# Two groups of dilated values projected together: 512 columns per strided stationary load, in two passes over h

## The chip, the cores and the metric

The kernel runs on 1 core of one Trainium2 chip. The metric is the device time of one execution in microseconds (us); lower is better. Each time shown is a run of the whole program; one further execution was recorded by the hardware profiler, and all rows below come from that one.

## The reference, cut to what matters

The program computes two transformer-like models in a row. Only the first is touched here: two layers over 512 tokens, each with a normed input h (512 x 1024), latent attention of 8 heads, and dilated attention of 8 heads in three groups.

```python
DIL_PAIRS = ((128, 1), (512, 4), (2048, 16))     # window, dilation
...
h = rms_norm(x, norm_g[layer])
p = h @ w_in[layer]
c_q, c_kv, k_r, gate_a, dil_qkv, gate_b = jnp.split(p, split_points, axis=-1)
a = mla_attention(c_q, c_kv, k_r, ...) * jax.nn.silu(gate_a)
b = dilated_attention(dil_qkv, cos_d, sin_d) * jax.nn.silu(gate_b)
x = x + jnp.concatenate([a, b], axis=-1) @ w_out[layer]
...
qkv = dil_qkv.reshape(B, S, DIL_GROUPS, 3, DIL_HEADS, DIL_HD)
for g, (window, dil) in enumerate(DIL_PAIRS):
    ...
    v = qkv[:, :, g, 2]
    o, lse = banded_attention(to_strided(q, dil), to_strided(k, dil), to_strided(v, dil), window // (2 * dil))
```

The values v of a group are a plain product of h with 512 columns of `w_in` (8 heads of 64). Groups 1 and 2 want them with the tokens in strided order.

## The kernel before, in words

All products of the first model are made of exact splits: a number is a high part plus a low part, and `mm3` (lines 346 to 351) issues three matmuls for each pair of operands, high by high at line 349, high by low at 350 and low by high at 351. The normed input lies feature-major in two tiles named `big` (high and low), 8 chunks of 128 features by 512 tokens. Each matmul has its own load of the stationary operand, which the profile lists as PEld LDWEIGHTS. A load takes 128 tokens by 128 features; the moving operand is the weights, in tiles `whi` and `wlo`.

`vproj(half)` projects the dilated values of four heads (256 columns) of each group. A call of `tile(g, i)` makes one tile of 128 tokens: 8 chunks by 3 matmuls of 256 columns into a PSUM bank of tag `mm` (three banks). For group 0 the tokens are 128 neighbours. For groups 1 and 2 they are every fourth token from i on, so the stationary load reads `big` with a step of four elements, 16 bytes. The first tile of a group also calls `k.weights` twice: each call is a DMA of 512 KB, a copy on ScalarE (line 400, the high part) and a subtraction on VectorE (line 401, the low part). ScalarE empties the bank at line 620 (groups 1 and 2) or 624 (group 0).

```python
sl = slice(i, 512, 4) if g else slice(i * P, (i + 1) * P)
for c in range(8):
    w, o = ws[g][c // 4], (c % 4) * 256
    k.mm3(acc[:, 0:256], tok(c, sl), (w[0][:, o : o + 256], w[1][:, o : o + 256]), c == 0, c == 7)
```

The steps of `vproj` are (cost, step) pairs. In each layer `v0` (first four heads) gives four steps ahead of the transposition of the latents (`latent`, lines 712 to 718), two more between those transpositions, and the rest to the first two of eight fills; `v1` gives four steps to the fourth fill and eight to the sixth. A fill is spread by `weave` between eight units of attention: `scores` (scores on TensorE, minimum on VectorE, exponential on ScalarE, scale on VectorE), and two units later `transposed`. TensorE and SyncE run in the order of the program text; for ScalarE, VectorE and GpSimd a scheduler orders the instructions. VectorE also carries work of the second model that `k.weights` pulls in, one step per call as a rule: products with `in_mw` at lines 953 and 954. `values` multiplies the finished values with the attention's weights, much later. Tiles of tag `v4` (ten slots) hold the values.

Of the kernel before, what the change touches and what calls it, by code (L numbers as in the profile page):

```python
# [30 lines left out]
# ---------------------------------------------------------------- host side  # L31
def _kp(w):
    """[K, N] -> [128, K/128, N], row k*128+p at partition p."""
    k, n = w.shape
    return w.reshape(k // P, P, n).transpose(1, 0, 2)
# [16 lines left out]
def layout(inp):  # L52
    """Rearranges the inputs' elements (copies only)."""
# [7 lines left out]
    for L in range(2):  # L61
# [3 lines left out]
        for half in range(2):  # L65
            for g in range(3):
                c0 = 1184 + ((g * 3 + 2) * 8 + 4 * half) * 64
                vs.append(wk[:, :, c0 : c0 + 256])
# [97 lines left out]
def constants():  # L166
    """Tables that depend on shapes alone."""
# [62 lines left out]
# tags of what outlives block 1's attention, and of what the even mixer starts with  # L230
# [3 lines left out]
# (t, g): t = 0 for q, 1 for k  # L234
# [4 lines left out]
# ---------------------------------------------------------------- chip side  # L239
class Phase:  # L240
    """Opens the pools of one stretch of the program, in the order of their bytes:
    one for each list of tags and, unless it is None, one for the rest."""
# [27 lines left out]
class K:  # L270
# [17 lines left out]
    def t(self, shape, tag, bufs, dt=F32):  # L288
        """A tile of the current phase's pool (weights: of the common pool)."""
        pool = self.sb if tag in ("wraw", "whi", "wlo", "cath", "catl") else self.two if tag == "big" else self.of.get(tag, self.pool)  # L290
        return pool.tile(shape, dt, tag=tag, bufs=bufs, name=self.nm(tag))
# [9 lines left out]
    def arrive(self, halves=2):  # L301
        """The next tile of x, or half of it, leaves the part before."""
        for _ in range(halves):
            if self.tail is not None:
                next(self.tail, None)

    def norms(self, first, rest):
        """first(i), then rest(i) of its result, for the tiles of x as they arrive."""
        self.arrive()
        self.arrive()  # L310
        a = first(0)
        self.arrive()
        b = first(1)
        self.arrive()
        for i in range(4):
            rest(i, a)
            a, b = b, first(i + 2) if i < 2 else None
# [5 lines left out]
    # ---- weights  # L323
# [5 lines left out]
    def weights(self, src, off, n, gate=None, raw=None, sub=None, tag=None):  # L329
        """Columns off.. of a weight array, loaded and split exactly into hi + lo."""  # L330
# [15 lines left out]
    def mm3(self, out, lhs, rhs, first, last):  # L346
        """out (+)= lhs^T rhs with lhs, rhs = (hi, lo)."""
        mm = self.nc.tensor.matmul
        mm(out, lhs[0], rhs[0], start=first, stop=False)  # L349
        mm(out, lhs[0], rhs[1], start=False, stop=False)  # L350
        mm(out, lhs[1], rhs[0], start=False, stop=last)  # L351

    def fm(self, w, nk, rhs):
        """Feature-major product: 128 columns of w against all tokens."""
# [6 lines left out]
    def copy(self, out, in_):  # L361
        """PSUM evacuation, alternating between the two engines that can."""
# [6 lines left out]
    def rsqrt(self, ss, n, eps=True):  # L369
        """[128, n] mean squares -> 1/sqrt(. + eps)."""  # L370
# [35 lines left out]
    def norm_steps(self, xn, hT, i):  # L406
        """xn [128 tokens, 1024] -> hT[:, :, tokens of tile i], split."""
# [18 lines left out]
def both(*gens):  # L426
    """Their steps in turn."""
    for _ in zip_longest(*gens):
        pass


def slow(gen, n):
    """Its steps with n - 1 empty ones after each."""
# [5 lines left out]
def weave(units, fill):  # L439
    """Emits the units with the fill's (cost, step) pairs spread evenly between them."""  # L440
# [9 lines left out]
def block1_layer(k, L, x, hT):  # L450
# [3 lines left out]
    # ---- norm and transposition  # L454
# [9 lines left out]
    def wc_weights(half):  # L464
        """The first chunks lie in other slots: they are split before the last part's end."""
# [84 lines left out]
    # Steps of dense work, as (cost, step): they fill the attention's waits.  # L550

    # ---- dilated q and k of a pair of heads, feature-major, with rope
# [51 lines left out]
    # ---- dilated values of four heads, token-major  # L604
    def vproj(half):
# [3 lines left out]
        def tile(g, i):  # L609
            if i == 0:  # L610
                base = (half * 3 + g) * 2048
                ws[g] = [k.weights(I["wv"][L], base + c * 1024, 1024) for c in range(2)]
                vs[g] = t([P, 4, 256], "v4", 10)
            acc = k.bank("mm")
            sl = slice(i, 512, 4) if g else slice(i * P, (i + 1) * P)
            for c in range(8):
                w, o = ws[g][c // 4], (c % 4) * 256
                k.mm3(acc[:, 0:256], tok(c, sl), (w[0][:, o : o + 256], w[1][:, o : o + 256]), c == 0, c == 7)
            if g:
                nc.scalar.activation(vs[g][:, i, :], acc[:, 0:256], AF.Copy, scale=0.5)  # L620
            else:
                # tile i holds tokens 128 i - 64 .. 128 i + 63, wrapped
                for src, dst in ((0, 64), (64, 0)):
                    nc.scalar.activation(vs[g][dst : dst + 64, (i + (src > 0)) % 4, :], acc[src : src + 64, 0:256], AF.Copy, scale=0.5)

        return [(2.6, lambda g=g, i=i: tile(g, i)) for g in (1, 2, 0) for i in range(4)]

    def gate(which, hp):
        """2 * silu(h w_gate) of a pair of heads, feature-major."""
# [29 lines left out]
    def proj(hp):  # L659
        """Queries and keys of a pair of latent heads, with their rope rows."""  # L660
# [30 lines left out]
    # ---- latent projections  # L691
# [36 lines left out]
    # rope of the shared key part  # L728
# [16 lines left out]
    # ---- latent values and the rope part of q  # L745
# [28 lines left out]
    # ---- attention: 64 units, first the latent heads', then the dilated heads'  # L774
# [3 lines left out]
    def softmax(pr, bias, src):  # L778
        """pr = exp(bias - src) / sum."""
# [57 lines left out]
    def values(p):  # L837
        """Of both heads of a pair, in turn: they take different columns of the array."""
# [7 lines left out]
        else:  # L846
            vs = vss[hp // 2]
            for g in (1, 2):
                for r in range(4):
                    for o, PT, hc in halves:  # L850
                        nc.tensor.matmul(
                            o[:, r * P : (r + 1) * P],
                            vs[g][:, r, hc],
# [67 lines left out]
def adaln(k, rows):  # L921
    """Modulation vectors of both layers (and the context's), as rows in DRAM;
    a generator, so that its steps lie between those of other work."""
# [52 lines left out]
def rms(k, src, tag=None):  # L976
    """1/rms of [128, 1024] rows; returns (scratch tile, [128, 1])."""
# [13 lines left out]
def new_cat(k, last=False):  # L991
    """A pair of blocks of w_out's left operand, split; the phase's last outlives it."""
# [24 lines left out]
def token_acc(k, ws, lhs, nk, acc=None, c0=None):  # L1017
    """lhs^T w over nk chunks of 128, or the four from c0; ws: split chunks of 4 * 256."""
# [22 lines left out]
def ctx_steps(k):  # L1041
    """The context's keys, transposed, and values, into DRAM: (cost, step) pairs."""
# [53 lines left out]
def twice(k, dst, src):  # L1096
    """Both halves of the partitions of dst = src, split."""
# [5 lines left out]
def even_mixer(k, x, rows):  # L1103
# [4 lines left out]
    # ---- the first part's last norm, the mixer's norm, and transposition  # L1108
# [5 lines left out]
    def squares(i, engine):  # L1114
        """Of x, and of x fg, which replaces it."""
# [10 lines left out]
    def rms(i):  # L1126
        """x r1 fg normed again has 1/rms = r1 rsqrt(r1^2 mean(u^2) + eps)."""
# [27 lines left out]
    # ---- keys, values, queries: T holds heads k0 k1 q0 .. q7  # L1155
# [4 lines left out]
    def finish(h0, nh):  # L1160
        """Gains, rope and norm of heads h0 .. h0+nh-1."""
# [74 lines left out]
    # ---- pooled branch  # L1236
# [5 lines left out]
    def pool_means(b, w=None):  # L1242
# [5 lines left out]
        # the window's width w times (mean - p): pool_scale is divided by w  # L1248
# [36 lines left out]
    # ---- attention: 32 units (pair of heads, tile of queries, head of the pair)  # L1285
# [40 lines left out]
    def values(u):  # L1326
        """Of both heads of a pair, whose second unit is u."""
# [22 lines left out]
    # ---- the order of the work  # L1350
# [35 lines left out]
def odd_mixer(k, x, rows):  # L1386
# [14 lines left out]
    # spatial gating operand, token-major, normed per group  # L1401
# [60 lines left out]
def router(k, L):  # L1462
    """The router's weights, and the shift's part of its logits."""
# [17 lines left out]
def moe_tables(k, L, rows):  # L1481
    """What an expert layer reads that does not depend on its input."""
# [8 lines left out]
def moe(k, L, x, tables, out):  # L1491
# [9 lines left out]
    # ---- router: x A is routed, and 1 / rms and the shift's part come to its logits  # L1501
# [19 lines left out]
    def logits(i):  # L1521
        """Four groups of the array's columns take two chunks each; their sums are added in turning them."""
# [40 lines left out]
    def route(i):  # L1563
        """Ranks within the groups' logits and within each group's experts', and the chosen two."""
# [23 lines left out]
    def before(i):  # L1588
        """How many tokens come before tile i's in their experts' lists."""
# [4 lines left out]
    def spots(i, n):  # L1594
        """The places of the tokens in their experts' lists less 256: in bfloat16, positive if not chosen."""
# [11 lines left out]
    def places(dst, e_pos, e_info, c0=0, c1=5, oh=None):  # L1607
        """One-hot matrix of each slot's token against token numbers and its weight's parts."""
# [9 lines left out]
    def indices(src, n, nm):  # L1618
        """[128, n, 2] sums -> the slots' tokens (out of bounds for an empty slot)."""
# [33 lines left out]
    def weigh():  # L1653
        """Each choice's weight, halved (the experts' activation comes doubled), in three exact parts."""
# [46 lines left out]
    def gate_up(e):  # L1701
        """The chunks of an expert's first two products."""
# [30 lines left out]
    def hidden(gu):  # L1733
        """2 silu(gate) up."""
# [84 lines left out]
    def store(y, gi):  # L1819
        """The tokens' rows += y."""  # L1820
# [32 lines left out]
    # ---- experts with more than 128 tokens: the rest of their lists  # L1853
# [53 lines left out]
    for e in range(15):  # L1907
        if e == 3 and out is None:
            # the last expert's slots, token by token
# [20 lines left out]
    # ---- the tokens' rows, what the last expert adds to them, and the odd mixer's norm  # L1930
# [44 lines left out]
def body(tc, I, out, stop=None):  # L1975
    nc = tc.nc
    with (
# [21 lines left out]
        with k.phase("two"):  # L1999
            k.two = k.pool  # L2000
            with tc.manual_schedule(engines={mybir.EngineType.PE, mybir.EngineType.SP}):
# [14 lines left out]
                # block 1's last steps and the even mixer's first ones overlap  # L2016
# [52 lines left out]
```

## Time and profile before

| | |
|---|---|
| median of 3 runs | 1963.19 us (1962.71 to 1967.38) |
| span of the profiled execution | 1966.2 us |
| TensorE busy | 1821.8 us, 93% |
| VectorE busy | 1342.3 us, 68% |
| ScalarE busy | 773.4 us, 39% |
| GpSimd busy | 276.5 us, 14% |

The profiled execution's own time is its span, 1966.2 us; it lies 3.0 us above the median of the runs and inside their range. A busy TensorE says that some matmul was under way, not that it ran at its best pace: matmuls are pipelined, their ends are modelled, and the pace of a stream is read from start to start.

### The profile page before, as it was taken

Reading aid. Unit: us, or ns where it says so; the run is one execution under the profiler, and the core shown is the slowest. Engines: PE = TensorE matmul, PEld = TensorE weight load, DVE = VectorE, ACT = ScalarE, POOL = GpSimd, SP = SyncE. Lnnn points to the kernel's source line nnn. Section 1 sums busy time; section 2 is a strip of 40 time slices with the busy share of each in tenths; the row PEclk is TensorE's granted clock in tenths of the full one; section 3 lists DMA queues with packets and bytes.
Section 4 is the critical chain, followed back from the end, with each engine's and each line's share of the span. In section 5 each row is a group of like instructions: output and inputs, shape, how many; then the busy total and the mean of one; then the engine's idle time right before and its main releaser. Section 6 shows DMA issues by size and latency. Waiting matters only on the chain. (4 is left out here: it accounts for less than half of the span.)

```text
span 1966.2 us, 26503 instructions
## 1 busy us (share of the span) xinstructions
PE 1821.8 (93%) x9926; PEld 1432.4 (73%) x9926; DVE 1342.3 (68%) x2516; ACT 773.4 (39%) x1361; POOL 276.5 (14%) x242
## 2 busy tenths in 40 slices
PE   7999999999989999999999788896999699978996
PEld 7986787797689777877877676684666487756664
DVE  4457667865653577556556778888978675678774
ACT  4244333333333443232243444553555332234552
POOL 0000000000120000000000345104222221223221
PEclk9999999999999999999999888998999899989998
DMA  4245556535211445355441322306898553248983
GB/s 166 76 132 143 152 149 208 179 109 174 60 43 54 141 134 154 115 166 155 120 128 41 104 74 75 117 1 223 319 338 281 177 202 110 64 172 304 333 309 82
DMA packets 86951, 298.95 MB, mean 152 GB/s; under 512 B 18854, under 2 KB 20694, under 8 KB 78624
## 3 DMA queue, kind: packets, MB, share of 16 engines
q1 hardware_dynamic: 71584, 271.87, 41.9%
q0 software_dynamic: 10704, 19.79, 4.4%
q10 hardware_dynamic: 4528, 5.51, 1.1%
q8 instruction: 81, 1.33, 0.3%
q14 instruction: 54, 0.44, 0.1%
HBM read 280.23 MB, written 24.96 MB: 155 GB/s over the span
## 5 line engine op out<-in xcount | busy, mean ns | idle before, releaser
L401 DVE TENSOR_TENSOR wlo<-wraw,whi 128x1024 fp32r<-128x1024 f32 (+3 forms) x165 | 204.3, 1239 | 175.7 <-ACT whi L400 163.0
L400 ACT ACTIVATE whi<-wraw 128x1024 fp32r<-128x1024 f32 (+2 forms) x166 | 171.5, 1035 | 376.0 <-PE psmm L350 252.9
L349 PE MATMUL psmm<-big,whi 128*128 128x512 f32 x672 | 271.7, 404 | 0.7 <-ACT e L1251 0.7
L350 PE MATMUL psmm<-big,whi 128*128 128x512 f32 x672 | 266.0, 396 | 0.0
L351 PE MATMUL psmm<-big,wlo 128*128 128x512 f32 x672 | 265.8, 395 | 0.0
L350 PE MATMUL psmm<-wlo,big 128*128 128x256 f32 (+1 forms) x624 | 210.1, 337 | 4.4 <-DVE wlo L401 4.3
L349 PE MATMUL psmm<-whi,big 128*128 128x256 f32 (+1 forms) x624 | 212.8, 341 | 1.0 <-ACT big L400 1.0
L351 PE MATMUL psmm<-whi,big 128*128 128x256 f32 (+1 forms) x624 | 210.1, 337 | 2.4 <-DVE big L401 2.4
L954 DVE CUSTOM_DVE_ANT_0 wraw<-wraw,sB 128x1024 f32<-128x1024 f32 x96 | 117.3, 1222 | 67.8 <-DMA wraw<-in_mw_dram 67.1
L350 PEld LDWEIGHTS psmm<-wlo,big 128*128 128x128 f32 x624 | 156.4, 251 | 5.0 <-DVE wlo L401 5.0
L351 PEld LDWEIGHTS psmm<-whi,big 128*128 128x128 f32 x624 | 156.1, 250 | 3.4 <-DVE big L401 3.4
L349 PEld LDWEIGHTS psmm<-whi,big 128*128 128x128 f32 x624 | 155.8, 250 | 2.0 <-ACT big L400 1.6
L351 PEld LDWEIGHTS psmm<-big,wlo 128*128 128x128 f32 x672 | 126.5, 188 | 30.8
L349 PEld LDWEIGHTS psmm<-big,whi 128*128 128x128 f32 x672 | 126.7, 188 | 28.9 <-ACT e L1251 0.9
L350 PEld LDWEIGHTS psmm<-big,whi 128*128 128x128 f32 x672 | 126.8, 189 | 27.8
L1839 PE MATMUL psmm<-wraw,hs 128*128 128x512 f32 x256 | 120.7, 613 | 5.7 <-ACT hs L1831 3.8
L600 POOL DMA_DIRECT2D qk<-rope x40 | 20.3, 511 | 715.1 <-DVE rope L598 306.2
L349 PE MATMUL pss<-whi,xTh 128*128 128x512 f32 x256 | 104.6, 409 | 1.5 <-ACT xTh L400 1.5
L351 PE MATMUL pss<-whi,xTl 128*128 128x512 f32 x256 | 102.1, 399 | 1.7 <-DVE xTl L401 1.7
L350 PE MATMUL pss<-wlo,xTh 128*128 128x512 f32 x256 | 103.4, 404 | 0.0
L830 PEld LDWEIGHTS pspt<-c_ident,pr 128*128 128x128 f32 x512 | 59.3, 143 | 49.1 <-issue 25.7
L401 DVE TENSOR_TENSOR wlo<-bigm,whi 128x1024 fp32r<-128x1024 f32 x64 | 78.0, 1223 | 17.8 <-ACT whi L400 16.7
(385 smaller groups left out, 3715.8 us busy)
## 6 DMA issues: line engine op xcount, KB each, us to landing
wraw<-in_mw_dram SPq DMA_DIRECT2D x96, 512.0 KB, 3.9
big<-in_me_dram SPq DMA_DIRECT2D x32, 1024.0 KB, 7.9
bigm<-in_me_dram SPq DMA_DIRECT2D x32, 1024.0 KB, 9.1
wraw<-in_me_dram SPq DMA_DIRECT2D x64, 512.0 KB, 7.2
wraw<-in_wqk_dram SPq DMA_DIRECT2D x48, 512.0 KB, 3.7
wraw<-in_wv_dram SPq DMA_DIRECT2D x24, 512.0 KB, 3.7
wraw<-in_ow_dram SPq DMA_DIRECT2D x20, 512.0 KB, 4.2
wraw<-in_wg_dram SPq DMA_DIRECT2D x16, 512.0 KB, 3.7
```

The source lines that it names most:

```text
L349: mm(out, lhs[0], rhs[0], start=first, stop=False)
L350: mm(out, lhs[0], rhs[1], start=False, stop=False)
L351: mm(out, lhs[1], rhs[0], start=False, stop=last)
L400: self.nc.scalar.activation(hi, src, AF.Copy)
L401: (sub or self.nc.vector).tensor_tensor(lo, src, hi.bitcast(F32), ALU.subtract)
L600: nc.gpsimd.dma_start(tiles[b][48:80, :], R[b // 4][32 * (b % 4) : 32 * (b % 4) + 32, :])
L830: nc.tensor.transpose(pt[:, j * P : (j + 1) * P], hd.pr[i][:, j * P : (j + 1) * P], ident)
L954: nc.vector.tensor_tensor_reduce(w, w, sB, 1.0, 0.0, ALU.mult, ALU.add, mf[:, j : j + 1])
L1839: nc.tensor.matmul(acc, hs[:, c * P : (c + 1) * P], w[:, c * 512 : (c + 1) * 512], start=c == 0, stop=c == 1)
```

## The change

The weights of groups 1 and 2 are laid side by side on the host: 512 columns per chunk of features. One half of `vproj` now goes in three parts: `pair(0, i)` takes chunks 0 to 3 of h for both groups, 512 columns to a full bank, and ScalarE copies the bank, halved, to SBUF; `pair(1, i)` takes chunks 4 to 7, and VectorE adds its bank, halved, to what lies in SBUF; `tile(i)` is group 0 as before. The number of steps, the places where they are handed to the fills, and the bytes of weights stay as they were; the cost of a step for `weave` goes from 2.6 to 2.8. The two tiles of values, 128 x 2 x 512, are taken when part 0 begins. Docstrings were dropped too, so that line numbers after differ.

```diff
-            for g in range(3):
-                c0 = 1184 + ((g * 3 + 2) * 8 + 4 * half) * 64
-                vs.append(wk[:, :, c0 : c0 + 256])
+            cols = [1184 + ((g * 3 + 2) * 8 + 4 * half) * 64 for g in range(3)]
+            vs.append(np.concatenate([wk[:, :, c0 : c0 + 256] for c0 in cols[1:]], axis=2))
+            vs.append(wk[:, :, cols[0] : cols[0] + 256])
...
-        def tile(g, i):
+        def pair(part, i):
             if i == 0:
-                base = (half * 3 + g) * 2048
-                ws[g] = [k.weights(I["wv"][L], base + c * 1024, 1024) for c in range(2)]
-                vs[g] = t([P, 4, 256], "v4", 10)
+                base = half * 6144 + part * 2048
+                ws[part] = [k.weights(I["wv"][L], base + c * 1024, 1024) for c in range(2)]
+                if part == 0:
+                    vs[1] = [t([P, 2, 512], "v4", 10) for _ in range(2)]
             acc = k.bank("mm")
-            sl = slice(i, 512, 4) if g else slice(i * P, (i + 1) * P)
-            for c in range(8):
-                w, o = ws[g][c // 4], (c % 4) * 256
-                k.mm3(acc[:, 0:256], tok(c, sl), ..., c == 0, c == 7)
-            if g:
-                nc.scalar.activation(vs[g][:, i, :], acc[:, 0:256], AF.Copy, scale=0.5)
+            for c in range(4):
+                w, o = ws[part][c // 2], (c % 2) * 512
+                k.mm3(acc, tok(4 * part + c, slice(i, 512, 4)), (w[0][:, o : o + 512], w[1][:, o : o + 512]), c == 0, c == 3)
+            dst = vs[1][i // 2][:, i % 2, :]
+            if part == 0:
+                nc.scalar.activation(dst, acc, AF.Copy, scale=0.5)
+            else:
+                nc.vector.scalar_tensor_tensor(dst, acc, 0.5, dst, op0=ALU.mult, op1=ALU.add)
...
-        return [(2.6, lambda g=g, i=i: tile(g, i)) for g in (1, 2, 0) for i in range(4)]
+        return ([(2.8, lambda p=p, i=i: pair(p, i)) for p in range(2) for i in range(4)]
+                + [(2.8, lambda i=i: tile(i)) for i in range(4)])
...
-                            vs[g][:, r, hc],
+                            vs[1][r // 2][:, r % 2, (g - 1) * 256 + hc.start : (g - 1) * 256 + hc.stop],
```

On TensorE, in the sixth fill of layer 0, the first step of `v1` that it holds comes behind a block of queries and keys (out `psmm`, stationary `whi`) and ahead of a unit's scores (`pss`). Before, the tile has 24 matmuls of 256 columns:

```order
L351 MATMUL psmm_3317<-big_77,wlo_3309 128x512
L349 MATMUL psmm_3390<-whi_3369,big_77 128x256
L350 MATMUL psmm_3390<-wlo_3370,big_77 128x256
L351 MATMUL psmm_3390<-whi_3369,big_78 128x256
...
L349 MATMUL psmm_3390<-whi_3380,big_77 128x256
L350 MATMUL psmm_3390<-wlo_3381,big_77 128x256
L351 MATMUL psmm_3390<-whi_3380,big_78 128x256
...
L810 MATMUL pss_3416<-k_566_2735,qk_2437 32x256 x4
```

At the same place after it has 12 of 512 columns, and the second weight tile (`whi_3237`) is read from the seventh on, where it was the thirteenth:

```order
L352 MATMUL psmm_3174<-big_77,wlo_3166 128x512
L350 MATMUL psmm_3246<-whi_3226,big_77 128x512
L351 MATMUL psmm_3246<-wlo_3227,big_77 128x512
L352 MATMUL psmm_3246<-whi_3226,big_78 128x512
...
L350 MATMUL psmm_3246<-whi_3237,big_77 128x512
L351 MATMUL psmm_3246<-wlo_3238,big_77 128x512
L352 MATMUL psmm_3246<-whi_3237,big_78 128x512
...
L824 MATMUL pss_3260<-k_567_2592,qk_2294 32x256 x4
```

On VectorE, in the same fill, the rows from the split of the next part's weights (`wlo`) on, with the minimum of the scores under the mask (`pr,mn`), the rope's products (`rope`), and the split that follows. Before:

```order
L401 TENSOR_TENSOR wlo_3540<-wraw_3537,whi_3539 128x1024
...
L819 ISA pr_3424,mn_3417<-pss_3416,dil_mask 128x512
...
L597 TENSOR_TENSOR rope_3245<-rope_3245,v_698_3347 32x512
...
L954 ISA wraw_3543,mod_1097<-wraw_3543,sB_940 128x1024
...
L598 TENSOR_TENSOR rope_3245<-rope_3245,rope_3354 64x512
...
L819 ISA pr_3497,mn_3490<-pss_3489,dil_mask 128x512
...
L401 TENSOR_TENSOR wlo_3551<-wraw_3548,whi_3550 128x1024
L401 TENSOR_TENSOR wlo_3714<-wraw_3711,whi_3713 128x1024
```

After, the four additions of part 1 (line 625, out and in `v_461` and `v_462`) stand between them, one behind the rope's products, and two products of line 954 went ahead of these rows:

```order
L402 TENSOR_TENSOR wlo_3348<-wraw_3345,whi_3347 128x1024
L625 SCALAR_TENSOR_TENSOR v_461_2091<-psmm_3246,v_461_2091 128x512
L833 ISA pr_3268,mn_3261<-pss_3260,dil_mask 128x512
...
L598 TENSOR_TENSOR rope_3102<-rope_3102,v_699_3204 32x512
...
L625 SCALAR_TENSOR_TENSOR v_461_2091<-psmm_3281,v_461_2091 128x512
L599 TENSOR_TENSOR rope_3102<-rope_3102,rope_3211 64x512
...
L625 SCALAR_TENSOR_TENSOR v_462_2092<-psmm_3295,v_462_2092 128x512
L833 ISA pr_3317,mn_3310<-pss_3309,dil_mask 128x512
...
L402 TENSOR_TENSOR wlo_3359<-wraw_3356,whi_3358 128x1024
L625 SCALAR_TENSOR_TENSOR v_462_2092<-psmm_3331,v_462_2092 128x512
L402 TENSOR_TENSOR wlo_3522<-wraw_3519,whi_3521 128x1024
```

The evictions of these four tiles, which ScalarE held before at line 620, are gone from its queue there.

## Rows read from the trace of the kernel before

**Rows 1.** The page: busy us of each engine (share of span).

```profile
span 1966.2 us, 26503 instructions
...
PE 1821.8 (93%) x9926; PEld 1432.4 (73%) x9926; DVE 1342.3 (68%) x2516; ACT 773.4 (39%) x1361; POOL 276.5 (14%) x242
```

**Rows 2.** By windows: stretch, length, busy PE, PEld, DVE, ACT, POOL (x); clock, DMA.

```profile
51.25:73.92 22.67, 22.64 (x98) 22.44 (x97) 8.96 (x32) 4.50 (x10) 0.00 (x0) 1.00 0.24 78
254.60:282.00 27.40, 27.40 (x122) 25.64 (x121) 16.21 (x28) 7.42 (x16) 3.29 (x6) 1.00 0.38 108
395.00:431.00 36.00, 36.00 (x192) 33.36 (x189) 21.94 (x39) 9.21 (x18) 2.98 (x6) 1.00 0.31 89
948.70:975.00 26.30, 26.30 (x133) 24.98 (x132) 11.42 (x22) 6.01 (x12) 2.15 (x5) 1.00 0.26 78
87.00:117.00 30.00, 26.66 (x131) 21.56 (x130) 15.98 (x23) 12.34 (x23) 0.41 (x4) 0.94 0.39 117
```

**Rows 3.** Timeline, TensorE, tile of group 1: start us, us, engine, line.

```profile
255.43 0.40 PE L349 MATMUL psmm<-whi,big 128*128 128x256 f32 x1
255.66 0.40 PE L350 MATMUL psmm<-wlo,big 128*128 128x256 f32 x1
...
260.09 0.40 PE L351 MATMUL psmm<-whi,big 128*128 128x256 f32 x1
```

**Rows 4.** Timeline, TensorE, a tile of group 0.

```profile
132.61 0.28 PE L350 MATMUL psmm<-wlo,big 128*128 128x256 f32 x1
...
135.20 0.28 PE L351 MATMUL psmm<-whi,big 128*128 128x256 f32 x1
```

**Rows 5.** Timeline, stationary loads behind an idle TensorE: strided, then not strided.

```profile
51.63 0.31 PEld L350 LDWEIGHTS psmm<-wlo,big 128*128 128x128 f32 x1 [0.23 <-DVE wlo L401]
51.84 0.33 PEld L351 LDWEIGHTS psmm<-whi,big 128*128 128x128 f32 x1
...
642.45 0.19 PEld L350 LDWEIGHTS psmm<-wlo,v 128*128 128x128 f32 x1 [2.02 <-DVE wlo L401]
642.56 0.19 PEld L351 LDWEIGHTS psmm<-whi,v 128*128 128x128 f32 x1
```

**Rows 6.** Timeline, a block of 512 columns and the tile behind it.

```profile
396.97 0.39 PE L349 MATMUL psmm<-big,whi 128*128 128x512 f32 x1
...
401.63 0.40 PE L351 MATMUL psmm<-big,wlo 128*128 128x512 f32 x1
...
401.64 0.31 PEld L349 LDWEIGHTS psmm<-whi,big 128*128 128x128 f32 x1
...
401.87 0.28 PE L349 MATMUL psmm<-whi,big 128*128 128x256 f32 x1
```

**Rows 7.** Timeline, ScalarE's evictions and VectorE's gate (in brackets: idle before).

```profile
62.92 0.38 ACT L620 ACTIVATE v<-psmm 128x256 f32<-128x256 f32 x1 [5.22 <-PE psmm L351]
...
388.02 0.58 ACT L571 ACTIVATE qk<-psmm 128x512 f32<-128x512 f32 x1
...
288.84 0.68 DVE L635 SCALAR_TENSOR_TENSOR gc<-gc,psmm 128x512 f32<-128x512 f32 x1
```

**Rows 8.** Timeline, VectorE and ScalarE in the sixth fill of layer 0.

```profile
409.38 3.37 DVE L597 TENSOR_TENSOR rope<-rope,v 32x512 f32<-32x512 f32 x4
...
421.76 0.69 DVE L819 CUSTOM_DVE_ANT_0 pr<-pss,dil_mask 128x512 f32<-128x512 f32 x1 [5.55 <-PE pss L817]
...
425.15 1.06 ACT L400 ACTIVATE whi<-wraw 128x1024 fp32r<-128x1024 f32 x1 [1.84 <-PE psmm L351]
...
426.24 1.23 DVE L401 TENSOR_TENSOR wlo<-wraw,whi 128x1024 fp32r<-128x1024 f32 x1 [1.44 <-ACT whi L400]
```

**Rows 9.** Timeline, VectorE and ScalarE under the first four tiles of layer 0.

```profile
58.81 0.35 DVE L706 TENSOR_SCALAR PT<-PT,rs_yn 128x256 f32<-128x256 f32 x1
...
71.32 1.06 ACT L400 ACTIVATE whi<-wraw 128x1024 fp32r<-128x1024 f32 x1 [2.42 <-PE psmm L351]
...
72.41 1.23 DVE L401 TENSOR_TENSOR wlo<-wraw,whi 128x1024 fp32r<-128x1024 f32 x1 [13.25 <-ACT whi L400]
```

More of the change, by code (lines that the diff above doesn't have):

```diff
@@ L614, in tile @@
             acc = k.bank("mm")
-            sl = slice(i, 512, 4) if g else slice(i * P, (i + 1) * P)
-            for c in range(8):
-                w, o = ws[g][c // 4], (c % 4) * 256
-                k.mm3(acc[:, 0:256], tok(c, sl), (w[0][:, o : o + 256], w[1][:, o : o + 256]), c == 0, c == 7)
-            if g:
-                nc.scalar.activation(vs[g][:, i, :], acc[:, 0:256], AF.Copy, scale=0.5)
-            else:
-                for src, dst in ((0, 64), (64, 0)):
-                    nc.scalar.activation(vs[g][dst : dst + 64, (i + (src > 0)) % 4, :], acc[src : src + 64, 0:256], AF.Copy, scale=0.5)
@@ new lines, in tile @@
+        def tile(i):
+            if i == 0:
+                base = half * 6144 + 4096
+                ws[2] = [k.weights(I["wv"][L], base + c * 1024, 1024) for c in range(2)]
+                vs[0] = t([P, 4, 256], "v4", 10)
+            acc = k.bank("mm")
+            for c in range(8):
+                w, o = ws[2][c // 4], (c % 4) * 256
+                k.mm3(acc[:, 0:256], tok(c, slice(i * P, (i + 1) * P)), (w[0][:, o : o + 256], w[1][:, o : o + 256]), c == 0, c == 7)
+            for src, dst in ((0, 64), (64, 0)):
+                nc.scalar.activation(vs[0][dst : dst + 64, (i + (src > 0)) % 4, :], acc[src : src + 64, 0:256], AF.Copy, scale=0.5)
@@ L628, in gate @@
+        return [(2.8, lambda p=p, i=i: pair(p, i)) for p in range(2) for i in range(4)] + [(2.8, lambda i=i: tile(i)) for i in range(4)]
     def gate(which, hp):
```

## The prediction

> **What bounds the kernel now.** I read the page first: the busy shares say that TensorE runs for 93% of a span of 1966.2 us and VectorE for 68% [rows 1]. A busy share tells only where to look, so next come stretches of the view by windows around the places where the dilated values are projected [rows 2]. The reader is to see that TensorE has no hole there (22.64 of 22.67 us, 27.40 of 27.40, 36.00 of 36.00, 26.30 of 26.30, clock 1.00), while ScalarE is under a third busy and VectorE between 8.96 of 22.67 and 21.94 of 36.00. What ends last in these stretches is TensorE, so its pace is what must be read, and that is read from the timeline, from start to start.
>
> In a tile of group 1 or 2 a matmul of 256 columns starts every 0.233 us: the 4th of a tile at 255.43, the 24th at 260.09, 4.66 us over 20 [rows 3]. In a tile of group 0, with the same 256 columns but tokens that lie side by side, it is 0.118 us (132.61 to 135.20 over 22) [rows 4]. The moving operand is the same, so the strided tile does not wait for columns: it waits for the stationary load. The load's record says so too, 0.33 us against 0.19 [rows 5]. Two places show a load with TensorE idle ahead of it [rows 5]. Strided, the load behind it is let in after 0.21 us (51.63, 51.84); not strided, after 0.11 us (642.45, 642.56). So a strided load holds the load path for 0.21 us by itself and 0.233 in the stream, and a 256-column matmul of 0.118 us lies hidden under it. Per load, half of the time gives no column.
>
> **The change, step by step.** There are 32 tiles of the two groups (2 layers, 2 halves, 2 groups, 4 tiles). Each has 8 chunks x 3 matmuls = 24; after, there are again 32 tiles, of 4 chunks x 3 = 12, now of 512 columns. So 768 strided loads become 384, and the columns stay the same.
>
> What does a 512-column matmul with a strided load cost? Without the stride, one starts every 0.233 us (396.97 to 401.63 over 20) [rows 6]. That is the same as the strided load's pace, and both lie on different work, so the pair costs about the larger of the two if they overlap. One row shows just this pair: at the end of a block of queries and keys a 512-column matmul starts at 401.63, the strided load of the next tile runs from 401.64 for 0.31, and the next matmul starts at 401.87 [rows 6]. The step is 0.24 us, no longer than the others in the block. I take 0.236. From below it cannot be under 0.233. From above: the load went from 0.213 alone to 0.233 with a stream of 0.118 beside it, 0.020 more; with a stream twice as long beside it this could be 0.040, so 0.253.
>
> A tile then costs 24 x 0.2333 = 5.60 us now and 12 x 0.236 = 2.83 after; what its first and last matmul cost beyond the pace is the same in both. That is 2.77 us a tile, **88.6 us** for 32. With 0.233 it is 89.7, with 0.253 it is 82.0.
>
> ScalarE loses 32 evictions of 256 columns (0.38 us each) and gets 16 of 512 (0.58, from an eviction of queries) [rows 7]: 12.2 us become 9.3, beside TensorE; it idled 5.22 us ahead of one of them. VectorE gets 16 additions that read PSUM, multiply and add 128x512. The nearest row has the same operation on the same shape, the gate at line 635, 0.68 us [rows 7]: 10.9 us in all. Their cover is VectorE's idle time, 14.06 of 36.00 us in 395.00:431.00. If the cover were gone, they would cost these 10.9 us.
>
> Is it gone? That stretch holds four of the tiles, so it shrinks by 4 x 2.77 = 11.1 to 24.9 us, and VectorE's part grows by 2.7 to 24.6. In 254.60:282.00 there are four more tiles, without additions: 16.3 us are left for 16.21. So VectorE loses nearly all its slack in these two stretches of layer 0; in layer 1 it keeps it (11.42 + 2.7 in 15.2). It helps that part of this work (the products of line 954 and their like) is wanted only much later, and that VectorE's gaps now are waits for TensorE itself (5.55 us at 421.76, for the scores) [rows 8], which come sooner when TensorE is faster. What is late next would be the rope's four products (3.37 us at 409.38): an addition of the second tile stands behind them in the new order, and its bank is held meanwhile. There are three banks and a tile takes 2.8 us, so 5.6 us are covered. I put 1 to 3 us on these stretches.
>
> The early tiles cover a chain: the norms of the latents. VectorE ends it at 58.81 + 0.35 = 59.16 and then idles 13.25 us [rows 9]. The first four tiles now last from 51.25 to 73.9; after, they end near 51.63 + 4 x 2.9 = 63.2. The chain still has 4 us to spare. The second weight chunk of the next part can be split only when the fourth tile has read its first chunk: the copy starts at 71.32 and VectorE's half ends at 73.64, 2.32 us. After, that is freed 6 x 0.236 = 1.4 us ahead of the tile's end, so it is ready 0.9 us behind it; eight transposes and six matmuls come first, over 2 us. Nothing waits. The weights of the last part follow the same pattern: the copy at 425.15 and the split to 427.47 begin at the middle of a tile [rows 8], again 2.3 us, and are wanted 1.4 us behind its end, at the earliest. The waits on w2 and on the first weights of the attention (26.66 of 30.00 us busy in 87.00:117.00) [rows 2] hang on slots that TensorE itself frees; they move, and do not shrink or grow. The DMA queues carry the same transfers in the same order.
>
> The sum: 88.6 less 3 us for VectorE's tight stretches is 85.6 us. The profiled execution's span, 1966.2 us, comes to 1880.6; it lies 3.0 us above the median of the runs, 1963.19, so **1877.6 us** is forecast.
>
> A rule against the change stands in the Trainium skill, "TensorE: Matmul & The Clock Gate", Part 3, The mechanism: a load overlaps matmuls in flight only when it goes to another group of rows. All loads here take all 128 rows, so by the rule load and stream would add up, 0.213 + 0.233 = 0.446 us a pair, and a tile would gain 0.25 us. The trace does not bear it out: pairs of 0.233 us hold a load that alone takes 0.11 or 0.21 [rows 3, 5, 6]. The same page, Part 2, LDWEIGHTS, gives a load by its columns alone (128 / 1.2 = 107 ns); by that figure the tiles now would run at their stream's 0.118 us and the change would gain nothing. The loads that are not strided agree with it (0.11), the strided ones do not (0.21).
>
> **Rivals.** (a) No overlap at 512 columns: the load waits for the stream. For it: no row shows two such pairs behind each other. Against it: the pair at 401.63 [rows 6]. A pair would take 0.446 us, a tile would gain 5.60 - 5.35 = 0.25, the whole 8 us less the 3: 1958. Half-way, at 0.35, the gain is 32 x 1.4 - 3 = 42 us: 1921.
> (b) VectorE becomes the bound of the dense stretches. For it: the 24.6 of 24.9 us above. If half of the 14.1 and 11.2 us that it idles there now stays, because the order of its queue is fixed, layer 0 loses 12.6 us instead of 3, and layer 1 some 5 more: 1877.6 + 15 = 1892.
> (c) Slower: the 16 banks that VectorE empties. When it stands behind work that waits for TensorE, TensorE waits for the bank, and both wait in turn. It decides from 85.6 / 16 = 5.4 us a tile on. The longest piece of VectorE's work there is the 3.37 us [rows 8], and two more banks cover 5.6 us. It would end near 1970, if each tile waited 5.8 us.
>
> **How the numbers follow.** My forecast with its own range, 1873 to 1887 (pace 0.233 to 0.253 us, 1 to 6 us of leaks), has 0.78. Rival (b), 1887 to 1900, has 0.11. Half-way overlap, near 1921, has 0.06; no overlap 0.03; slower 0.02. The range that leaves out no more than 2 in 10 reaches from 1871 into rival (b), 1895; the rest stays outside. A measurement of this kernel can tell about 0.3% (5.9 us) from no change. Faster by more than that are the forecast, (b) and half-way: 0.95 and a part of no overlap, 0.96 in all; 0.02 within; 0.02 slower.
>
> **What would show it.** In the profile after: 384 strided loads under 512-column matmuls, a start every 0.23 to 0.25 us; tiles of 2.9 us; the first four tiles over near 63; no new wait of TensorE for a bank in its list of waits; VectorE's additions at 0.68 us. The prediction is wrong if the pairs start 0.3 us apart or more, if TensorE waits for VectorE in the stretches of layer 0 by more than 10 us in all, or if the clock falls below 1.00 in them because gaps open.

## The result, and the profile after

The changed kernel takes 1881.46 us (median of 4 runs, 1877.5 to 1883.23); the kernel before, run again with it, 1962.95 (4 runs, 1960.73 to 1967.38). The ratio is 0.9582 with a 95% interval of 0.9566 to 0.9598: faster by 81.5 us. The forecast was 1877.6, range 1871 to 1895.

The page of the kernel after, which answers to [rows 1]: TensorE has 384 matmuls and 384 loads less and is busy 82.6 us less; VectorE is busy 8.2 us more.

```profile
span 1878.8 us, 25737 instructions
...
PE 1739.2 (93%) x9542; PEld 1346.2 (72%) x9542; DVE 1350.5 (72%) x2532; ACT 772.9 (41%) x1345; POOL 279.5 (15%) x242
```

The same stretches of the program as in [rows 2], by windows (same columns); they begin and end at the same places of the program as there, to some 0.3 us:

```profile
50.16:62.14 11.98, 11.98 (x51) 11.62 (x50) 7.89 (x32) 5.17 (x10) 0.00 (x0) 1.00 0.45 148
232.18:249.00 16.82, 16.82 (x74) 14.91 (x73) 15.26 (x27) 8.05 (x15) 3.16 (x6) 1.00 0.46 124
361.74:387.00 25.26, 25.26 (x143) 22.34 (x140) 21.73 (x39) 7.67 (x14) 2.99 (x6) 1.00 0.40 112
873.37:889.30 15.93, 15.93 (x86) 14.32 (x86) 12.26 (x25) 4.65 (x9) 2.15 (x5) 1.00 0.44 113
```

Each holds four tiles. The reader is to see that TensorE fills all four (its busy time is their length, clock 1.00), as it did before, and that they are shorter by 10.69, 10.58, 10.74 and 10.37 us, which is 2.59 to 2.69 us a tile. VectorE is nearly as busy in the second as TensorE (15.26 of 16.82), and still TensorE has no hole.

A tile behind the transposes of a unit, on the timeline of TensorE, and the first of its stationary loads:

```profile
236.49 0.60 PE L350 MATMUL psmm<-whi,big 128*128 128x512 f32 x1
236.92 0.40 PE L351 MATMUL psmm<-wlo,big 128*128 128x512 f32 x1
237.16 0.39 PE L352 MATMUL psmm<-whi,big 128*128 128x512 f32 x1
...
239.31 0.40 PE L352 MATMUL psmm<-whi,big 128*128 128x512 f32 x1
```

```profile
236.46 0.31 PEld L350 LDWEIGHTS psmm<-whi,big 128*128 128x128 f32 x1
236.67 0.33 PEld L351 LDWEIGHTS psmm<-wlo,big 128*128 128x128 f32 x1
236.92 0.31 PEld L352 LDWEIGHTS psmm<-whi,big 128*128 128x128 f32 x1
```

From the 2nd to the 12th matmul 2.39 us pass, 0.239 a step. That is 0.006 us more than the strided load's pace in [rows 3], with twice the columns over it. The first step is longer, 0.43: two loads follow each other after 0.21, and only then, as we read it, does the first stream run, beside the second of them.

Read over all 32 tiles in this way, from the start of the first matmul to the start of what comes behind the last, they take 181.13 us before and 96.18 after: 84.95 us less. From the first tile to the first product of the second model (called the block below) it is 1065.92 and 982.84: 83.1 us less. So the gain lies in the tiles.

### The profile page after: what moved, and what is told of

Its sections match the earlier page's. It is cut to its first block, busy times and chain, and to the rows that moved or that the text cites. A ratio compares the mean times of both kernels' runs of the same rounds, so it can differ in the third digit from the quotient of the medians.

```text
span 1878.8 us, 25737 instructions
## 1 busy us (share of the span) xinstructions
PE 1739.2 (93%) x9542; PEld 1346.2 (72%) x9542; DVE 1350.5 (72%) x2532; ACT 772.9 (41%) x1345; POOL 279.5 (15%) x242
## 5 line engine op out<-in xcount | busy, mean ns | idle before, releaser
L350 PE MATMUL psmm<-whi,big 128*128 128x256 f32 (+2 forms) x496 | 165.3, 333 | 1.0 <-ACT big L401 1.0
L351 PE MATMUL psmm<-wlo,big 128*128 128x256 f32 (+2 forms) x496 | 160.7, 324 | 4.7 <-DVE wlo L402 4.7
L352 PE MATMUL psmm<-whi,big 128*128 128x256 f32 (+2 forms) x496 | 160.1, 323 | 2.4 <-DVE big L402 2.3
L351 PEld LDWEIGHTS psmm<-wlo,big 128*128 128x128 f32 x496 | 112.2, 226 | 5.8 <-DVE wlo L402 5.6
L352 PEld LDWEIGHTS psmm<-whi,big 128*128 128x128 f32 x496 | 111.5, 225 | 3.2 <-DVE big L402 3.2
L350 PEld LDWEIGHTS psmm<-whi,big 128*128 128x128 f32 x496 | 111.7, 225 | 2.0 <-ACT big L401 1.6
```

## The experiments

In e1, e2, e4, e5 and e7 the values of the first model are others than the reference's, and other values send more than 128 tokens to some experts of the second model. A loop for the rest of their lists, which neither before nor after runs, then adds over 1000 us, as the costliest line of e1 shows:

```profile
L1882 PE MATMUL pss<-wraw,wraw 128*128 128x512 f32 x768 | 413.7, 688 | 14.7 <-DMA wraw<-in_me_dram 14.0
```

Their totals (3090 to 4339 us) say nothing of the change. They are read by the 32 tiles and by the block, both of which lie ahead of that loop. The table holds these readings for all kernels, worked out from the starts of matmuls in each trace (a first step is from the first matmul's start to the second's, the pace that of the other steps, both medians):

| kernel | 32 tiles, us | first step | pace | block, us | total, us |
|---|---|---|---|---|---|
| before | 181.13 | 0.319 | 0.233 | 1065.92 | 1962.95 |
| after | 96.18 | 0.434 | 0.238 | 982.84 | 1881.46 |
| e1, before, not strided | 92.69 | 0.200 | 0.118 | 975.12 | |
| e2, after, not strided | 90.64 | 0.313 | 0.229 | 980.03 | |
| e3, two additions | 96.17 | 0.433 | 0.237 | 980.49 | 1882.95 |
| e4, no addition | 96.16 | 0.433 | 0.237 | 980.35 | |
| e5, 384 columns in half the steps | 94.57 | 0.433 | 0.234 | 981.64 | |
| e6, before in two passes | 181.11 | 0.319 | 0.233 | 1065.17 | 1965.84 |
| e7, before, step of two | 95.32 | 0.206 | 0.120 | 980.53 | |
| e8, scores last in a unit | 97.50 | 0.434 | 0.237 | 1000.91 | 1897.81 |

**e1: does the stride set the pace before?**

```diff
-            sl = slice(i, 512, 4) if g else slice(i * P, (i + 1) * P)
+            sl = slice(i * P, (i + 1) * P)
```

> The kernel before, but the tiles of groups 1 and 2 load 128 neighbouring tokens instead of every fourth (so these two groups get values of other tokens); 24 matmuls of 256 columns a tile as before, no second pass, no addition. My theory, that the strided load alone set the pace of these tiles: the pace falls from 0.233 to 0.118 us, a tile from 5.66 to 2.9 us, the whole by 32 x 2.75 = 88 us to about 1876 us, a few us under the changed kernel (1881). Rival, that the gain came from fewer matmuls and loads issued or from the new order of ScalarE and VectorE: no such gain, 1955 to 1963 us.

Measured: the block is 90.8 us shorter with not a column less. On the timeline the 2nd and the 24th matmul of one tile stand 2.49 us apart, 0.113 a step (the median over all tiles is 0.118):

```profile
233.08 0.28 PE L350 MATMUL psmm<-wlo,big 128*128 128x256 f32 x1
...
235.57 0.28 PE L351 MATMUL psmm<-whi,big 128*128 128x256 f32 x1
```

So the strided load set the pace, and nothing else held these tiles.

**e2: what of the stride is left after?**

```diff
-                k.mm3(acc, tok(4 * part + c, slice(i, 512, 4)), ...)
+                k.mm3(acc, tok(4 * part + c, slice(i * P, (i + 1) * P)), ...)
```

> The changed kernel with neighbouring tokens in the two passes (values of other tokens again). My theory, that a pair of strided load and 512-column matmul costs the larger of the two, which are nearly equal: the pace falls only from 0.238 to 0.233 us and the start of a tile by 0.1 us, so 32 x 0.15 = 5 us, 1876 us. Rival, that load and stream still hinder each other at 512 columns: more than 10 us, under 1871. Rival, that the columns alone count: no difference, 1881.

Measured: the tiles take 90.64 us, 5.5 less than after: the pace goes from 0.238 to 0.229, the first step from 0.434 to 0.313. On the timeline:

```profile
233.40 0.48 PE L350 MATMUL psmm<-whi,big 128*128 128x512 f32 x1
233.72 0.40 PE L351 MATMUL psmm<-wlo,big 128*128 128x512 f32 x1
...
236.01 0.39 PE L352 MATMUL psmm<-whi,big 128*128 128x512 f32 x1
```

The change has turned a stride that cost 88.4 us in the tiles (before less e1) into one that costs 5.5.

**e3 and e4: do the additions on VectorE cost anything?** e3 does each twice (a quarter of the bank each time), e4 none: there ScalarE copies part 1 over part 0. In e3:

```diff
-                nc.vector.scalar_tensor_tensor(dst, acc, 0.5, dst, op0=ALU.mult, op1=ALU.add)
+                for _ in range(2):
+                    nc.vector.scalar_tensor_tensor(dst, acc, 0.25, dst, op0=ALU.mult, op1=ALU.add)
```

and in e4:

```diff
-                nc.vector.scalar_tensor_tensor(dst, acc, 0.5, dst, op0=ALU.mult, op1=ALU.add)
+                nc.scalar.activation(dst, acc, AF.Copy, scale=0.5)
```

> The changed kernel with each addition of part 1 done as two, each with a quarter of the bank, so that VectorE has 16 more operations of 0.68 us and each bank is held that much longer. My theory, that the additions lie in VectorE's waits: 0 to 3 us more, 1881 to 1884. Rival (b), that VectorE bounds the dense stretches: 11 us more or above, 1892.

> The changed kernel where ScalarE copies the bank of part 1 over that of part 0, so that the addition is left out (values of half the rows of h) and VectorE has none of the new work. My theory: 0 to 3 us less, 1878 to 1881. Rival (b): 8 to 11 us less, about 1871.

Measured: 1882.95 us for e3 (ratio to before 0.9591, 0.9568 to 0.9615; after has 0.9582), and with 32, 16 and 0 additions blocks of 980.49, 982.84 and 980.35. The additions, by line, in after and in e3:

```profile
L625 DVE SCALAR_TENSOR_TENSOR v<-psmm,v x16: 671/692/692, 66.2 to 889.1; 128x512 f32<-128x512 f32 x16
its engine sat idle before it (us, times) until:
  PE psmm L352: 5.2, 7
```

```profile
L626 DVE SCALAR_TENSOR_TENSOR v<-psmm,v x32: 671/691/692, 66.8 to 890.4; 128x512 f32<-128x512 f32 x32
```

They last what the gate lasted in [rows 7] (median 0.69 us), and ahead of 7 of the 16 VectorE waits for TensorE. Nothing waits for the additions of after; in e3 two stationary loads do, 0.5 us in all (from the same view). So even 22 us of additions stay hidden but for that, and the blocks show no trend with their number.

**e5: does the pair cost the larger of load and stream?** In the inner two of a tile's four chunks the matmuls take 384 columns.

```diff
+                n = 512 if c in (0, 3) else 384
-                k.mm3(acc, tok(...), (w[0][:, o : o + 512], w[1][:, o : o + 512]), ...)
+                k.mm3(acc[:, 0:n], tok(...), (w[0][:, o : o + n], w[1][:, o : o + n]), ...)
```

> The changed kernel where the matmuls of the second and third chunk of each part (6 of 12) take 384 of the 512 columns, so that a quarter of the values of the two groups lacks half of its rows. It reads the pace of a strided load under a shorter stream. If a pair costs the larger of load and stream, the load of 0.233 us sets it: the pace stays between 0.23 and 0.24 us, and the time at 1881. If load and stream add up in part, 128 columns (0.058 us) fewer show: 0.18 to 0.20 us, and 32 x 6 x 0.05 = 10 us less.

Measured: a quarter less columns in half of the matmuls, and from one of them to the next the step stays at a median of 0.232 us. On the timeline, from the first of the six on:

```profile
234.70 0.34 PE L350 MATMUL psmm<-whi,big 128*128 128x384 f32 x1
234.88 0.40 PE L351 MATMUL psmm<-wlo,big 128*128 128x384 f32 x1
235.11 0.39 PE L352 MATMUL psmm<-whi,big 128*128 128x384 f32 x1
235.34 0.40 PE L350 MATMUL psmm<-whi,big 128*128 128x384 f32 x1
235.58 0.40 PE L351 MATMUL psmm<-wlo,big 128*128 128x384 f32 x1
```

The first of the six steps is shorter, 0.18, and a step behind them is longer by as much (0.29), so a tile's total tells most: it fell by 0.05 us (94.57 against 96.18 over 32 tiles). If load and stream added up, six streams with 128 columns less would have taken some 0.35 us from it (estimated from 0.118 us for 256 columns). So below 512 columns the load sets the pace, as it did at 256. Wider is free until the stream is as long as the load, and 512 is about that point.

**e6: do the two passes bring anything by themselves?** Before, with a tile in two passes of four chunks, still at 256 columns; the first is copied, the second added.

```diff
-            acc = k.bank("mm")
-            for c in range(8):
+            for part in range(2 if g else 1):
+                acc = k.bank("mm")
+                cs = range(4 * part, 4 * part + 4) if g else range(8)
+                for c in cs:
...
+                if g and part == 0:
+                    nc.scalar.activation(vs[g][:, i, :], acc[:, 0:256], AF.Copy, scale=0.5)
+                elif g:
+                    nc.vector.scalar_tensor_tensor(vs[g][:, i, :], acc[:, 0:256], 0.5, vs[g][:, i, :], op0=ALU.mult, op1=ALU.add)
```

> The kernel before with the second half of the change alone: each tile of groups 1 and 2 in two passes of four chunks at 256 columns, the first copied by ScalarE, the second added on VectorE (32 additions of 128x256). As many strided loads as before. My theory: no gain, 1963 to 1966 us. Rival, that the two passes or the lighter ScalarE bring part of the gain: 1940 or below.

Measured: 1965.84 us, ratio 1.0007 (0.9992 to 1.0021), tiles 181.11. The passes, the second eviction and the additions neither cost nor bring anything; the whole gain is the width.

**e7: is a load's time proportional to its step?** Before, with every second token instead of every fourth.

```diff
-            sl = slice(i, 512, 4) if g else slice(i * P, (i + 1) * P)
+            sl = slice(256 * (i // 2) + i % 2, 256 * (i // 2) + 256, 2) if g else slice(i * P, (i + 1) * P)
```

> The kernel before with every second token of a half instead of every fourth of the whole (values of other tokens), a step of 8 bytes instead of 16. It prices the load by its step. If the price goes by the bytes that are passed over, the pace of 256-column tiles lies half way, at 0.16 to 0.18 us, 1963 - 45 = 1918 us. If only a step of 16 bytes costs, it is 0.118 us and 1876. If any step costs the same, 0.233 us and 1963.

Measured: a pace of 0.120 us and tiles of 95.32 us in all: 22 steps in 2.68 us on the timeline, with the load's own record at 0.19, as for loads without a stride [rows 5].

```profile
231.25 0.28 PE L350 MATMUL psmm<-wlo,big 128*128 128x256 f32 x1
...
233.93 0.28 PE L351 MATMUL psmm<-whi,big 128*128 128x256 f32 x1
```

A step of 8 bytes costs next to nothing, one of 16 bytes doubles the load. It isn't proportional.

**e8: can the tile's first load be hidden?** After, with a unit's scores issued behind its values and transposes, so that in most places a long stream precedes a tile, in place of short transposes.

```diff
-        if u < 64:
-            scores(u)
         if u >= 10 and u % 8 == 2:
             values(u // 8 - 1)
         if 2 <= u < 66:
             transposed(u - 2)
+        if u < 64:
+            scores(u)
```

> The changed kernel where a unit of attention issues its values and transposes first and its scores last, so that a tile's first strided load stands behind a long matmul instead of behind 128-column transposes. The step from the first to the second matmul of a tile is 0.43 us there, 0.20 above the pace, because the first load has nothing to hide under. My theory: in the tiles that follow a latent head's unit (half of those in the fills) it falls to 0.24; 10 tiles x 0.2 = 2 us less, and as much again for the blocks that follow units; 1877 us. Rival, that the scores come later and the softmax with them: no gain or a loss, 1881 to 1890.

Measured: 1897.81 us, ratio to before 0.9657 (0.9637 to 0.9678): 16 us slower than after, and slower than either expectation. Transposes now come before other work that stood ahead of them, and TensorE waits longer for the softmax. From the list of waits within the block, first after, then e8 (total us, times, longest):

```profile
PE pspt L844 <- DVE pr L798: 2.2, 1, 2.2
```

```profile
PE pspt L844 <- DVE pr L798: 6.7, 4, 1.8
```

That is 4.5 us more. In all, TensorE idles 3.75 us more in the block than in after (32.45 us, from the window below, against 28.70, from the window of after in the next section), of the 18 us by which it grew. It is also busy 14.3 us longer, at a lower granted clock:

```profile
49.59:1050.50 1000.91, 968.46 (x5334) 757.53 (x5332) 678.12 (x1292) 377.10 (x687) 54.75 (x79) 0.97 0.44 133
```

By the granted clock in the traces, TensorE is at the lower of its two levels, 1.2 GHz, for 58 us of this block, in after for 32. A step of 256 columns takes 0.21 us there instead of 0.12 (next section), so 26 us more of it are worth some 11 us, by estimate. Most of what the waits leave is thus accounted for by the clock; what lowered it wasn't tested. A tile's first step is no test here, since behind scores it also holds their stream.

## Why the prediction was right, step by step

**The strided load sets the pace of before: shown.** e1 takes the stride away and the tiles fall from 181.13 to 92.69 us with the same columns.

**A pair costs the larger of load and stream: shown.** 512 columns over a strided load step at 0.238 us, 384 at 0.232 (e5), 256 at 0.233 before, and 512 without the stride at 0.229 (e2). Rival (a), that the two add up to 0.446, falls, and so does the reading of the rule of the Trainium skill that stood behind it ("TensorE: Matmul & The Clock Gate", Part 3, The mechanism): loads of all 128 rows do run under the stream here.

**"What its first and last matmul cost beyond the pace is the same in both": this step was wrong in size, and with it the term of 88.6 us, which measured 84.95.** Behind short transposes no long stream covers a tile's first load. About 0.2 us of it lie open in both kernels, and then comes the first stream, 0.12 us before and 0.235 after: 0.32 and 0.43. Before, the sum had priced this step at the pace of 0.233, so it was 0.09 over; after, it is 0.20 over. Over all tiles the first step's mean went from 0.275 to 0.349 us, which takes 32 x 0.074 = 2.4 us from the gain. The pace takes another part: 0.2408 in the mean instead of the 0.236 that was taken (the range had 0.233 to 0.253), 32 x 10 x 0.0048 = 1.5 us, of which 0.3 comes back, since the pace of before was 0.2337 in the mean and not 0.2333. Together 3.6, and 88.6 - 84.95 = 3.65. The table supports the first part: without the stride the first step is 0.08 us over its stream in e1 and in e2, with it 0.20 both before and after.

**3 us for VectorE's tight stretches: the place was wrong.** The stretch that was to hold 24.6 us of VectorE in 24.9 holds 21.73 in 25.26, since the products of lines 953 and 954 of before take about 2.7 us less in it: part of them had gone ahead. The rope's products still stand where they were feared, behind the first addition and ahead of the second. From VectorE's timeline there:

```profile
371.67 0.69 DVE L625 SCALAR_TENSOR_TENSOR v<-psmm,v 128x512 f32<-128x512 f32 x1 [0.65 <-PE psmm L352]
...
375.39 3.40 DVE L598 TENSOR_TENSOR rope<-rope,v 32x512 f32<-32x512 f32 x4
...
378.91 0.67 DVE L625 SCALAR_TENSOR_TENSOR v<-psmm,v 128x512 f32<-128x512 f32 x1
```

The addition comes at 378.91, and TensorE went on through it with other banks. With the additions doubled, in e3, 22.38 us of VectorE lie in 26.00, and TensorE has one hole, of 0.21 us:

```profile
361.00:387.00 26.00, 25.79 (x141) 21.91 (x140) 22.38 (x42) 8.03 (x13) 2.98 (x6) 1.00 0.34 102
```

The hole is a wait for the split of the second weights of group 0. After has it too, in layer 1, 12 matmuls into the first tile of group 0, and before has none in either place:

```profile
890.95 0.38 PE L351 MATMUL psmm<-wlo,big 128*128 128x256 f32 x1 [0.51 <-DVE wlo L402]
```

So "Nothing waits" and the 2.3 us behind the middle of a tile were off by half a microsecond here: ScalarE, behind an exponential, begins the copy only at 888.35, about 1 us behind that middle, and VectorE, behind an addition, begins the split at 889.67. Rivals (b), VectorE as the bound, and (c), banks held back, did not come about: no wait of TensorE's matmuls in the block was ended by an addition.

**What was lost instead** is the 1.9 us between the tiles' 84.95 and the block's 83.1. It isn't more idle time. By the windows of the block, first before, then after, TensorE idles 29.36 us and 28.70:

```profile
51.25:1117.17 1065.92, 1036.56 (x5719) 830.78 (x5717) 668.95 (x1276) 381.35 (x703) 54.86 (x79) 0.99 0.42 125
```

```profile
50.16:1033.00 982.84, 954.14 (x5335) 744.99 (x5333) 677.04 (x1292) 379.99 (x687) 54.94 (x79) 0.98 0.46 136
```

What differs, beside single waits, is the granted clock. Between the tiles the same work is longer in three places (1.5, 1.2 and 1.8 us) and shorter in two (1.5 and 0.8). One of the longer ones lies in layer 1, behind the six early tiles, where TensorE waits twice for the latents' weights. From its timeline after:

```profile
578.89 0.38 PE L350 MATMUL psmm<-whi,v 128*128 128x256 f32 x1 [0.91 <-ACT whi L401]
581.09 0.58 PE L351 MATMUL psmm<-wlo,v 128*128 128x256 f32 x1 [1.82 <-DVE wlo L402]
...
581.69 0.41 PE L350 MATMUL psmm<-whi,v 128*128 128x256 f32 x1
581.90 0.41 PE L351 MATMUL psmm<-wlo,v 128*128 128x256 f32 x1
582.11 0.41 PE L352 MATMUL psmm<-whi,v 128*128 128x256 f32 x1
```

Waits like these were there before (1.81 us at 642.45, and 2.02 for its load in [rows 5]), with the clock at 1.00; after them the steps now are 0.21 us, where before had 0.12. The windows of both show the clock, first after, then before:

```profile
578.00:585.00 7.00, 4.29 (x21) 4.09 (x22) 4.36 (x6) 1.70 (x4) 0.00 (x0) 0.76 0.41 111
```

```profile
639.00:646.00 7.00, 4.27 (x32) 3.73 (x31) 4.36 (x6) 2.59 (x5) 0.00 (x0) 1.00 0.34 100
```

A mean of 0.76 is a stretch partly at the lower of the two levels, 1.2 GHz. This costs some 1.5 us (from the sixth tile's end to the seventh's start it is 31.63 us, before 30.09). The change is not what lowers it: e6, whose tiles are as long as those of before, has 31.45 us in that place, and its clock falls there too:

```profile
636.00:643.00 7.00, 4.27 (x23) 3.74 (x22) 4.36 (x6) 2.10 (x4) 0.00 (x0) 0.81 0.38 101
```

In the whole block TensorE is at the lower level for 26 us before, 32 after, 28 in e6 and 22 in e3 (by the granted clock in the traces). Why it is there in one execution and not in another wasn't tested. The blocks of after, e3 and e4 differ by 2.5 us among themselves, so a loss of 1.9 us is at the limit of what one profile can tell.

**The early chain: right.** The first four tiles were to end near 63.2; they ended at 62.14, having begun 1.1 us earlier than before; they last 11.98 us where 11.6 had been said. The latents' norms were to be ready 4 us ahead; VectorE ends them at 57.73 + 0.35 = 58.08, and is idle 3.92 us ahead of the next split, where it idled 13.25 in [rows 9]:

```profile
57.73 0.35 DVE L720 TENSOR_SCALAR PT<-PT,rs_yn 128x256 f32<-128x256 f32 x1
62.00 1.23 DVE L402 TENSOR_TENSOR wlo<-wraw,whi 128x1024 fp32r<-128x1024 f32 x1 [3.92 <-ACT whi L401]
```

**The sum.** Of the 3.9 us between 1877.6 and 1881.46, the tile term was 3.65 too large and the leak of 3 about 1.1 too large the other way; the block fell by 83.1 where 85.6 had been said. The other 1.4 us lie between the block of one execution (83.1) and the medians, which differ by 81.5, with 0.2 us the other way between the two medians of before; that is within the spread of the runs and stays unexplained.

## What to carry to other kernels

Where matmuls start at a steady pace that their columns don't explain, compare the same matmul with another stationary operand in the same trace: the difference is the load's, and it can be filled with columns up to the point where the stream is as long. Price a tile's first step apart from its pace, since its load has nothing to hide under and its own stream counts in full. An extra pass with an addition on another engine was all but free here, where the trace shows that engine waiting for the matmuls and not the other way round.

## What the hardware showed beyond that

The load's cost has a step between 8 and 16 bytes: paces of 0.118 us for neighbours, 0.120 for a step of 8 bytes (e7), 0.233 for 16. The Trainium skill, "SBUF — State Buffer", Specifications (TRN2), has lines of 16 bytes that want at least two accesses each for full bandwidth; e7 agrees, since it reads two values of each such line and before reads one. A later sentence of the page (Door 1: The DMA port swizzle), that four fp32 can be strided for free, does not hold for these loads: four fp32 are before's 16 bytes.

A strided load alone holds the load path for 0.21 us, and under a stream of 512 columns the pair came to 0.238 where the same stream without a stride had 0.229 (e2). So the larger of the two is not quite the whole of it: 0.009 us a pair remain that neither accounts for.
